# A temperature softmax over 32 x 512 x 1024: the first load in two pieces, and one store by Pool's queue

## The chip, the cores and the metric

The kernel runs on one core of one Trainium2 chip. The metric is the device time in microseconds (us) of one execution. The kernel before takes 317.71 us, the median of three runs (317.61 to 318.15).

## The reference

```python
batch, seq, dim = 32, 512, 1024      # x is float32, temperature is 0.5
def reference(x, temperature):
    scaled = x / temperature
    shifted = scaled - np.max(scaled, axis=-1, keepdims=True)
    exp_x = np.exp(shifted)
    return (exp_x / np.sum(exp_x, axis=-1, keepdims=True)).astype(np.float32)
```

It is a softmax over rows of 1024 numbers, 16,384 rows in all. Input and output are 67.11 MB each, and both have to pass through the core once.

## The kernel before, in words

The rows are cut into 16 tiles. A tile has 1024 rows, eight on each of the 128 partitions of the on-chip memory: 4 MiB. In memory the eight rows of a partition lie one after the other, so that a partition's part of a transfer is one run of 32,768 bytes. Six buffers hold tiles (BUFS = 6, L11), and each tile is worked on in place. It has two groups of four rows per partition (GROUP = 4, L13), 32 groups in all.

For a group, `maximum` (L64) finds the largest element of each row on DVE (L70, one instruction for four rows) and turns it into a bias (L73). `exponential` (L75) computes exp(scale * x + bias) on ACT, a row per instruction with the sum of the row beside it (L79). `divide` (L88) takes the reciprocals of the sums (L91) and multiplies the rows by them on DVE (L93). `store` (L97), after the second group of a tile, sends the tile to memory and calls `load` (L57) for the tile six further on, which takes the buffer that comes free.

Two things set the order of the work:

- The order of instructions on each engine is the order in which the program issues them (L107, a schedule by hand). First come six loads. Then for each group g: maximum and exponential of g, division of g - 1, store of g - 1. So on DVE the maximum of a group stands ahead of the division of the group before it. The division of a tile's second group therefore comes after the maximum over the first group of the next tile, which needs that tile to be loaded.
- All loads are issued by SP (L61). The seventh and later ones wait for a store to land, since they fill the buffer which it empties. All stores are issued by ACT (L101), between its exponentials. Each of the two issuing engines has a queue of its own to the 16 DMA engines, and each DMA engine serves both queues.

Pool (GpSimd) does nothing in this kernel but write four constants at the start.

Of the kernel before, what the change touches and what calls it, by code (L numbers as in the profile page):

```python
# [1 line left out]

# [4 lines left out]

TILES = [[8]] * 16  # L10
BUFS = 6  # L11

GROUP = 4  # L13


@with_exitstack
def kernel(
    ctx: ExitStack,
    tc: tile.TileContext,
    x: bass.AP,  # L20
    temperature: bass.AP,
    out: bass.AP,
):
    nc = tc.nc
    f32 = mybir.dt.float32
    scale = 1.0 / float(temperature)
    extreme = mybir.AluOpType.max if scale > 0 else mybir.AluOpType.min

    P = 128
    xf = x.flatten_outer_dims()  # L30
    of = out.flatten_outer_dims()
    n, d = xf.shape
    assert sum(sum(ks) for ks in TILES) * P == n

    data = ctx.enter_context(tc.tile_pool(name="data", bufs=BUFS))
    stats = ctx.enter_context(tc.tile_pool(name="stats", bufs=4))


    groups, first, r = [], [], 0
    for i, ks in enumerate(TILES):  # L40
        first.append(r)
        r += sum(ks)
        a = 0
        for k in ks:
            for b in range(0, k, GROUP):
                m = min(GROUP, k - b)
                groups.append((i, a + b, m, (a, k) if b + m == k else None))
            a += k

    def dram(t, i):  # L50
        k = sum(TILES[i])
        block = t[P * first[i] : P * (first[i] + k), :]
        return block.rearrange("(p k) d -> p k d", p=P, k=k)

    tiles, small = [], []

    def load():  # L57
        i = len(tiles)
        if i < len(TILES):
            xt = data.tile([P, sum(TILES[i]), d], f32, name="xt")  # L60
            nc.sync.dma_start(out=xt, in_=dram(xf, i))  # L61
            tiles.append(xt)

    def maximum(g):  # L64
        i, a, k, _ = groups[g]
        top, bias, sums, recip = (
            stats.tile([P, k], f32, name=name) for name in ("top", "bias", "sums", "recip")
        )
        small.append((bias, sums, recip))
        nc.vector.tensor_reduce(  # L70
            out=top, in_=tiles[i][:, a : a + k, :], axis=mybir.AxisListType.X, op=extreme
        )
        nc.vector.tensor_scalar_mul(bias, in0=top, scalar1=-scale)  # L73

    def exponential(g):  # L75
        i, a, k, _ = groups[g]
        bias, sums, _ = small[g]
        for b in range(k):
            nc.scalar.activation(  # L79
                tiles[i][:, a + b, :],  # L80
                tiles[i][:, a + b, :],
                mybir.ActivationFunctionType.Exp,
                bias=bias[:, b : b + 1],
                scale=scale,
                accum_out=sums[:, b : b + 1],
            )

    def divide(g):  # L88
        i, a, k, _ = groups[g]
        _, sums, recip = small[g]  # L90
        nc.vector.reciprocal(recip, sums)  # L91
        for b in range(k):
            nc.vector.tensor_scalar_mul(  # L93
                tiles[i][:, a + b, :], in0=tiles[i][:, a + b, :], scalar1=recip[:, b : b + 1]
            )

    def store(g):  # L97
        i, _, _, part = groups[g]
        if part:
            a, k = part  # L100
            nc.scalar.dma_start(out=dram(of, i)[:, a : a + k, :], in_=tiles[i][:, a : a + k, :])  # L101
            if a + k == sum(TILES[i]):
                load()

    with tc.manual_schedule():  # L107

        nc.vector.addr_align(128, offset=0, max_nops=0)
        nc.scalar.addr_align(128, offset=0, max_nops=0)  # L110
        for _ in range(BUFS):
            load()
        for g in range(len(groups) + 1):
            if g < len(groups):
                maximum(g)
                exponential(g)
            if g > 0:
                divide(g - 1)
                store(g - 1)


# [1 line left out]
_INS = ['x', 'temperature']  # L123
_OUTS = [((32, 512, 1024), 'float32')]

_NUMBERS = {'temperature': 0.5}


# [26 lines left out]
```

## Time and profile before

| | |
|---|---|
| median of three runs | 317.71 us |
| the profiled execution's own time | 317.42 us |
| its span, from first to last instruction | 315.6 us |
| DVE busy | 235.5 us (75%) |
| ACT busy | 149.6 us (47%) |
| Pool busy | 0.2 us |
| bytes read and written | 67.11 MB and 67.11 MB, 425 GB/s over the span |
| a load, from issue to landing | 12.7 us at least, 50.2 us in the median |
| a store, from issue to landing | 12.8 us at least, 38.4 us in the median |
| L70, the maximum of a group | 32 times, 4416 ns each |
| L93, a division of a row per partition | 128 times, 749 ns each |
| L79, an exponential of a row per partition | 128 times, 1137 ns each |

The span runs from the first to the last instruction; the device time has 1.8 us more around it. A line such as L61 is a line of the kernel's file. "Issue" of a DMA is the moment at which the engine hands it to its queue; "landing" is when its last byte is there and the waiting engines are told. A row of the waits gives the engine and line that waited, what it waited for, the sum in us, how often, and the longest. A row of the time order gives the start in us, the duration, engine, line, operation, and in brackets the idle time before it and what ended it. A row of the stretches gives the stretch, its length, the busy time of DVE, ACT and Pool with the number of instructions, the clock, the mean busy share of the 16 DMA engines and GB/s. Queue q1 is SP's, q10 is ACT's.

### The profile page before, as it was taken

Reading aid. Unit: us, or ns where it says so; the run is one execution under the profiler, and the core shown is the slowest. Engines: PE = TensorE matmul, PEld = TensorE weight load, DVE = VectorE, ACT = ScalarE, POOL = GpSimd, SP = SyncE. Lnnn points to the kernel's source line nnn. Section 1 sums busy time; section 2 is a strip of 40 time slices with the busy share of each in tenths; the row PEclk is TensorE's granted clock in tenths of the full one; section 3 lists DMA queues with packets and bytes.
Section 4 is the critical chain, followed back from the end, with each engine's and each line's share of the span. In section 5 each row is a group of like instructions: output and inputs, shape, how many; then the busy total and the mean of one; then the engine's idle time right before and its main releaser. Section 6 shows DMA issues by size and latency. Waiting matters only on the chain.

```text
span 315.6 us, 622 instructions
## 1 busy us (share of the span) xinstructions
DVE 235.5 (75%) x224; ACT 149.6 (47%) x257; POOL 0.2 (0%) x4
## 2 busy tenths in 40 slices
DVE  0299999999789494994939949498594976949720
ACT  0176666666626255361553615546065560645500
POOL 0000000000000000000000000000000000000000
DMA  8999999999999999999999999999999999999996
GB/s 330 415 448 415 386 457 407 461 411 453 424 440 432 432 432 429 444 424 453 415 454 407 457 407 457 403 461 403 461 403 461 403 462 403 461 419 444 428 436 278
DMA packets 4613, 134.26 MB, mean 425 GB/s; under 512 B 512, under 2 KB 512, under 8 KB 512
## 3 DMA queue, kind: packets, MB, share of 16 engines
q1 hardware_dynamic: 2304, 67.11, 49.7%
q10 hardware_dynamic: 2304, 67.11, 49.2%
q14 instruction: 5, 0.04, 0.0%
HBM read 67.11 MB, written 67.11 MB: 425 GB/s over the span
## 4 chain that ended last, share of the span: by engine, by line
DVE 72%; another core or an unknown queue 15%; DMA 4%; ACT 3%; issue 1%; DVEq 0%
DVE top L70 43%; DVE xt L93 27%; DMA xt<-in_x_dram 4%; ACT xt L79 3%; DVE recip L91 1%; DVE bias L73 1%; DVEq L150 0%
## 5 line engine op out<-in xcount | busy, mean ns | idle before, releaser
L79 ACT ACTIVATE xt<-xt,bias 128x1024 f32<-128x1024 f32 x128 | 145.4, 1137 | 136.0 <-DVE recip L91 118.6
L70 DVE TENSOR_REDUCE top<-xt 128x4 f32<-128x4096 f32 x32 | 141.3, 4416 | 62.2 <-DMA xt<-in_x_dram 62.2
L93 DVE TENSOR_SCALAR xt<-xt,recip 128x1024 f32<-128x1024 f32 x128 | 87.7, 749 | 1.1
L79 ACT ACTIVATION_READ_ACCUMULATOR xt<-xt,bias 128x1 f32 x128 | 23.8, 186 | 0.0
L79 ACT ACT_TABLE_LOAD x1 | 1.3, 1283 | 13.5 <-DMA xt<-in_x_dram 13.5
L91 DVE RECIPROCAL recip<-sums 128x4 f32<-128x4 f32 x32 | 5.5, 171 | 2.1 <-ACT xt L79 2.1
L73 DVE TENSOR_SCALAR bias<-top 128x4 f32<-128x4 f32 x32 | 5.5, 170 | 1.1
L136 POOL MEMSET const-bfloat16-1.0<- 128x1 bf16 x1 | 0.1, 102 | 0.0
L136 POOL MEMSET const-uint8-127<- 128x1 uint8 x1 | 0.1, 102 | 0.0
L136 POOL MEMSET const-float32-0.0<- 128x1 f32 x1 | 0.1, 99 | 0.2 <-issue 0.2
L136 POOL MEMSET const-float32-1.0<- 128x1 f32 x1 | 0.1, 99 | 0.0
## 6 DMA issues: line engine op xcount, KB each, us to landing
xt<-in_x_dram SPq DMA_DIRECT2D x16, 4096.0 KB, 50.2
out_dram<-xt ACTq DMA_DIRECT2D x16, 4096.0 KB, 38.4
```

The costliest lines, as they stand in the source:

```text
L70: nc.vector.tensor_reduce(out=top, in_=tiles[i][:, a : a + k, :], axis=mybir.AxisListType.X, op=extreme)
L73: nc.vector.tensor_scalar_mul(bias, in0=top, scalar1=-scale)
L79: nc.scalar.activation(tiles[i][:, a + b, :], tiles[i][:, a + b, :], mybir.ActivationFunctionType.Exp, bias=bias[:, b : b + 1], scale=scal ...
L91: nc.vector.reciprocal(recip, sums)
L93: nc.vector.tensor_scalar_mul(tiles[i][:, a + b, :], in0=tiles[i][:, a + b, :], scalar1=recip[:, b : b + 1])
L136: nc = _bacc.Bacc("TRN2", target_bir_lowering=False, num_devices=1)
```

## The change

Two edits. The load of tile 0 becomes two DMAs on SP's queue: one of partitions 0 to 15 (512 KiB), then one of partitions 16 to 127 (3.5 MiB). What needs tile 0 waits for both. The other 15 loads stay as they are. And the store of tile 8, one of 16, is issued by Pool's queue instead of ACT's; the wait for the last division of tile 8 goes with it. The load of tile 14, which takes tile 8's buffer, stays on SP and waits for that store to land, as before.

```diff
 GROUP = 4
+
+BY_POOL = 8
...
             xt = data.tile([P, sum(TILES[i]), d], f32, name="xt")
-            nc.sync.dma_start(out=xt, in_=dram(xf, i))
+
+            for p, q in ((0, 16), (16, P)) if i == 0 else ((0, P),):
+                nc.sync.dma_start(out=xt[p:q], in_=dram(xf, i)[p:q])
             tiles.append(xt)
...
         if part:
             a, k = part
-            nc.scalar.dma_start(out=dram(of, i)[:, a : a + k, :], in_=tiles[i][:, a : a + k, :])
+
+            queue = nc.gpsimd if i == BY_POOL else nc.scalar
+            queue.dma_start(out=dram(of, i)[:, a : a + k, :], in_=tiles[i][:, a : a + k, :])
             if a + k == sum(TILES[i]):
                 load()
```

## The prediction

> **What bounds the kernel now.** I read the DMA rows of the page first, then the stretches, then the waits, then the time order around tile 8 and at the end. The page:
>
> ```profile
> DMA  8999999999999999999999999999999999999996
> ...
> q1 hardware_dynamic: 2304, 67.11, 49.7%
> q10 hardware_dynamic: 2304, 67.11, 49.2%
> ```
>
> The reader is to see that the DMA engines have no free tenth between the first slice and the last. Loads are q1 (SP's queue), stores q10 (ACT's). Each queue has 2048 data packets of 32,768 B (67.11 MB) and 256 small completions. A store packet takes 49.2% x 16 x 315.6 us / 2048 = 1.213 us. An engine carries 256 packets in all: 256 x 1.213 = 310.5 us of a span of 315.6 us. The stretches say the same, with the share of the DMA engines in the last but one column:
>
> ```profile
> 0.00:2.00 2.00, 0.00 (x0) 0.00 (x0) 0.20 (x4) 1.00 0.61 168
> 2.00:33.00 31.00, 19.23 (x16) 13.18 (x22) 0.00 (x0) 1.00 1.00 427
> 33.00:173.00 140.00, 117.03 (x113) 73.62 (x127) 0.00 (x0) 1.00 1.00 431
> 173.00:282.00 109.00, 81.58 (x78) 53.49 (x94) 0.00 (x0) 1.00 1.00 433
> 282.00:302.00 20.00, 17.65 (x19) 9.27 (x16) 0.00 (x0) 1.00 0.97 419
> 302.00:313.00 11.00, 0.00 (x0) 0.00 (x0) 0.00 (x0) 1.00 0.99 429
> 313.00:316.00 3.00, 0.00 (x0) 0.00 (x0) 0.00 (x0) 1.00 0.08 33
> ```
>
> The waits show that the compute engines have time to spare in the long middle, and that what they lack is loaded tiles:
>
> ```profile
> DVE top L70 <- DMA xt<-in_x_dram: 62.2, 12, 13.4
> ```
>
> The first of these 12 waits (13.4 us) is the start; the others are 3 to 5 us, once a tile, from 84.8 us on. In the time order around tile 8:
>
> ```profile
> 173.65 0.34 ACTq L101 DMA_DIRECT2D out_dram<-xt  x1
> 173.91 19.67 SPq L61 DMA_DIRECT2D xt<-in_x_dram  x2
> ...
> 185.48 4.42 DVE L70 TENSOR_REDUCE top<-xt 128x4 f32<-128x4096 f32 x1 [4.48 <-DMA xt<-in_x_dram]
> ...
> 193.00 0.34 ACTq L101 DMA_DIRECT2D out_dram<-xt  x1
> ```
>
> The store of tile 8 is issued at 173.65 us; the load of tile 12 follows at 173.91 us, when the store of tile 6 has landed; tile 10 lands at 185.46; the store of tile 9 goes out at 193.00, 7.54 us after that landing. A store goes out 7.54 us after the landing of a later tile (store 9 after tile 10), since L70 of tile i+1 stands before the last division of tile i. Landings follow every 19.35 us, which is 16 packets of 1.213 us: one load packet, one store packet, in turn. At 173.65 store 7 has its whole tile still to send, so ACT's queue holds one full store in reserve. And the end:
>
> ```profile
> 282.25 4.42 DVE L70 TENSOR_REDUCE top<-xt 128x4 f32<-128x4096 f32 x1 [4.49 <-DMA xt<-in_x_dram]
> ...
> 302.01 0.34 ACTq L101 DMA_DIRECT2D out_dram<-xt  x1
> ```
>
> The last tile is there at 282.2, its store goes out 19.8 us later and lands 12.8 us after that (the least of all stores). So there are two bounds that almost coincide: the DMA work, which ends at 313 to 314.5 us, and the last load plus 33.4 us (315.6 - 282.25). The reserve of stores covers the DMA engines after the last load; nothing is left over. Whatever makes the last load later makes the end later.
>
> [...] The trace shows about 1.0 us for SP (issue at 0.73, first packet at 1.74); nothing of Pool's.
>
> **The change, part by part.** The sum is made against the profiled execution, 317.42 us: its span of 315.6 and 1.8 outside. It lies 0.1% below the median, 317.71.
>
> *The split of the first load.* One more issue on SP, 0.33 us (the row of L61 has 327 ns at least). Loads 1 to 5 are issued later by that, hidden under tile 0's 9.7 us of packets (8 x 1.213); uncovered it would cost 0.33. The 16 more completions are 4 bytes each: nothing. [...] Together 5.7 us, an estimate. Nothing takes it back, since the engines have no free time later: loads, stores and end move by it. Lower bound: zero, if packets are dealt by destination, so that engines not concerned go on with the 112 partitions. Below zero at most about 0.3 us, from a shorter first issue (0.52 against 0.33 us shown, the first of them cold). [...] I take 5.7.
>
> *The store of tile 8 on Pool's queue.* ACT loses one issue of 0.34 us, in a stretch where it waits 7.3 us a tile for DVE: worth nothing. Pool has 0.2 us of work in the whole span, so its wait for the division holds up nobody behind it. Its issue and descriptor work are not shown: [...] a late start only moves the same packets. The first of DVE's next operations is L70, 4.41 us, so nothing short is needed there.
> But it is moved past the store of tile 7: on ACT's queue it would wait behind it; on its own it sends at once. For its 8 packets an engine has three queues in turn, and a load packet comes every 3.64 instead of 2.43 us. Over 8 turns loads fall behind by 8 x 1.213 = 9.7 us. Tile 10 lands some 4.2 us late (3.5 packets left, each 1.21 later), tile 11 at 204.8 + 9.7 = 214.5. Stores come forward instead: store 7 ends about 201.9, store 9 follows directly, has 7 packets left when store 8 is done at 204, and ends at 204 + 7 x 2.43 = 221.3. Store 10 goes out at 214.5 + 7.54 = 222.0 and sends from 223.0. So ACT's queue is empty for 1.7 us, in which loads have the engines alone and win 1.7 us back. 8.0 us remain: store 11 goes out at 224.2 + 8.0 + 7.5 = 239.7 and store 10 is busy till 242.4, so both queues stay filled and the lag is carried to the last load, 290.2. Then the reserve is missing: store 13 ends at about 295, store 14 goes out at 290.2 + 7.5 = 297.7. The engines stand idle about 4 us, and again 2.5 us ahead of the last store. The chain gives the last load + 33.4 = 323.6 span, +8.0 us. Landing of store 8 at 205 rather than 212.6 lets load 14 be issued sooner, behind two others: worth nothing. Bounds: zero, if Pool's packets are served only when another queue is empty and tile 14 is not delayed; above, if they are small and take small turns: a ninth of a turn makes 64 turns of 2.6 us, the load of tile 14 waits for that landing, and the end comes at about +12.5. I take 8.0.
>
> Sum: 317.42 + 5.7 + 8.0 = 331.1 us.
>
> **The rivals.**
> *Pool only.* Packets dealt by destination, the split free: 317.4 + 8.0 = 325.4. [...]
> *Split only.* Pool's queue costs the loads nothing: 317.4 + 5.7 = 323.1. For it: nothing of Pool's is shown. Against: the equal turns of the other two queues.
> *Faster.* The engines do not end together: after 313 us a share of 0.08 over 3 us remains, and the packet records end between 313.3 and 314.5 us, so the last engine is one packet behind, and every landing waits for it. If the stretch in which ACT's queue is empty lets that engine catch up on loads, the last landing comes one packet sooner: 317.4 - 1.2 = 316.2. [...]
> *No change*, 317.4: Pool's packets come late and the split is free.
>
> **How the numbers follow.** Both costs 0.47 (329 to 335, with small turns of Pool's); Pool only 0.22; split only 0.14 (321 to 326); faster 0.08; no change 0.09, of which 0.06 within 0.2% and 0.03 slower. 0.2% is about what a measurement of this kernel tells from no change. So slower 0.47 + 0.22 + 0.14 + 0.03 = 0.86. The range leaves out faster, no change and the lowest of split only: 321.5 to 335.
>
> **What would show it.** Split: first landing (L70's first start, now 13.42) at 17 to 22 us, and tile 0's packets longer than 1.213 us; at 13.4 the split is free. Pool: three queues in the table; waits of L70 of 8 to 10 us for tiles 10 and 11 after 173 us, 4.5 again later; DMA tenths under 9 after the last load. If L70 keeps its 4.5 us and the last slices stay full, my step on turns is wrong. The prediction falls if both are so.

## The result, and the profile after

The changed kernel takes 329.77 us (median of five runs, 329.73 to 330.17), the kernel before 317.61 us beside it: a ratio of 1.0384, interval 1.037 to 1.0398. The forecast was 331.1. The profiled execution took 329.73 us with a span of 328.0, 12.4 us more than the span before.

The DMA rows of the page, kernel after:

```profile
DMA  8999999999999999999999999999999999997877
...
q1 hardware_dynamic: 2320, 67.11, 50.2%
q10 hardware_dynamic: 2160, 62.92, 44.5%
q0 software_dynamic: 144, 4.19, 3.0%
```

Two things have changed. The last four figures of the row are 7 and 8: engines stand idle there, where before only the last figure was below 8. And q1, the loads, took 50.2% of 328.0 us, 164.7 us per engine, where it was 49.7% of 315.6, 156.9 us, for the same bytes: load packets became 7.8 us longer in sum. Pool's queue q0 carries 144 packets, 128 of 32,768 B and 16 completions, so its packets have the size of the others; 3.0% of 328.0 us over 8 packets per engine is 1.23 us each, about the 1.213 of theirs.

The stretches of the kernel after (DMA share and GB/s in the last two columns):

```profile
2.00:8.00 6.00, 0.00 (x0) 0.00 (x0) 0.00 (x0) 1.00 0.81 132
8.00:22.00 14.00, 0.00 (x0) 0.00 (x0) 0.00 (x0) 1.00 0.99 269
22.00:173.00 151.00, 129.47 (x121) 84.64 (x145) 0.00 (x0) 1.00 1.00 433
...
296.00:316.00 20.00, 17.65 (x19) 9.27 (x16) 0.00 (x0) 1.00 0.75 323
316.00:328.00 12.00, 0.00 (x0) 0.00 (x0) 0.00 (x0) 1.00 0.82 350
```

From 8 to 22 us the engines are busy the whole time and move 269 GB/s instead of 427: not idle, but slow. From 296 to 316 us the packets have their usual length (1.216 us in the median) and the engines are idle a quarter of the time. So there are two costs of two kinds, one seen at each end of the kernel.

The time order, kernel after:

```profile
22.43 4.42 DVE L74 TENSOR_REDUCE top<-xt 128x4 f32<-128x4096 f32 x1 [22.43 <-DMA xt<-in_x_dram]
...
173.60 4.42 DVE L74 TENSOR_REDUCE top<-xt 128x4 f32<-128x4096 f32 x1 [4.49 <-DMA xt<-in_x_dram]
...
196.58 4.42 DVE L74 TENSOR_REDUCE top<-xt 128x4 f32<-128x4096 f32 x1 [8.11 <-DMA xt<-in_x_dram]
...
221.96 4.42 DVE L74 TENSOR_REDUCE top<-xt 128x4 f32<-128x4096 f32 x1 [10.52 <-DMA xt<-in_x_dram]
...
296.22 4.42 DVE L74 TENSOR_REDUCE top<-xt 128x4 f32<-128x4096 f32 x1 [4.46 <-DMA xt<-in_x_dram]
...
315.98 0.34 ACTq L107 DMA_DIRECT2D out_dram<-xt  x1
```

L74 here is L70 of before. These are the first maxima of tiles 0, 9, 10, 11 and 15, and the issue of the last store. Against before (13.42, 166.13, 185.48, 204.83, 282.25 us) they are late by 9.0, 7.5, 11.1, 17.1 and 14.0 us. The first lag is the split's. Pool's store, issued at 181.38 us, adds 3.6 at tile 10 and 9.6 at tile 11; later some of it is won back. From the last load to the end of the span are 31.8 us, 1.6 fewer than before: 14.0 - 1.6 = 12.4.

### The profile page after: what moved, and what is told of

It is laid out like the page before. It is cut to its first block, busy times and chain, and to the rows that moved or that the text cites. A ratio compares the mean times of both kernels' runs of the same rounds, so it can differ in the third digit from the quotient of the medians.

```text
span 328.0 us, 625 instructions
## 1 busy us (share of the span) xinstructions
DVE 235.5 (72%) x224; ACT 149.6 (46%) x257; POOL 0.9 (0%) x5
## 3 DMA queue, kind: packets, MB, share of 16 engines
q1 hardware_dynamic: 2320, 67.11, 50.2%
## 4 chain that ended last, share of the span: by engine, by line
DVE 48%; DMA 36%; another core or an unknown queue 8%; ACT 3%; issue 1%; DVEq 0%; SPq 0%
DVE top L74 29%; DMA xt<-in_x_dram 21%; DVE xt L97 17%; DMA out_dram<-xt 15%; ACT xt L83 3%; DVE bias L77 1%; DVE recip L95 1%; DVEq L156 0%; SPq L65 0%; DVEq L74 0%
## 5 line engine op out<-in xcount | busy, mean ns | idle before, releaser
L74 DVE TENSOR_REDUCE top<-xt 128x4 f32<-128x4096 f32 x32 | 141.3, 4416 | 76.1 <-DMA xt<-in_x_dram 76.1
L83 ACT ACT_TABLE_LOAD x1 | 1.3, 1283 | 22.4 <-DMA xt<-in_x_dram 22.4
L107 POOL DMA_DIRECT2D out_dram<-xt x1 | 0.7, 655 | 180.9 <-DVE xt L97 180.9
## 6 DMA issues: line engine op xcount, KB each, us to landing
xt<-in_x_dram SPq DMA_DIRECT2D x1, 3584.0 KB, 21.2
```

The lines of the kernel that those rows point to most:

```text
L74: nc.vector.tensor_reduce(out=top, in_=tiles[i][:, a : a + k, :], axis=mybir.AxisListType.X, op=extreme)
L83: nc.scalar.activation(tiles[i][:, a + b, :], tiles[i][:, a + b, :], mybir.ActivationFunctionType.Exp, bias=bias[:, b : b + 1], scale=scal ...
L107: queue.dma_start(out=dram(of, i)[:, a : a + k, :], in_=tiles[i][:, a : a + k, :])
```

## The experiments

**One part at a time, and two other cuts of the first load.** e1 has only the split, by setting the number of the tile that goes by Pool to none.

```diff
-BY_POOL = 8
+BY_POOL = None
```

> Only the split of the first load (16 and 112 partitions); all stores by ACT. [...] the packets of tile 0 last longer, as in the changed kernel, where the loads' packets took 7.8 us more per DMA engine (50.2% of 328.0 us against 49.7% of 315.6), and nothing takes it back: 317.6 + 7.8 = 325.4 us, first maximum at about 22.4 us, waits of L74 4.5 us in the middle. The prediction's own figure was 323.1. Rival, the two edits only hurt together (the split costs its place in time, the lag vanishes once stores begin): under 320.

Measured: 325.51 us against 317.9, ratio 1.0233 (1.0218 to 1.0249), +7.6. The last load is 8.0 us late, as tile 9 is already 7.8 us late: what the start costs is not given back.

e2 has only the store by Pool.

```diff
-            for p, q in ((0, 16), (16, P)) if i == 0 else ((0, P),):
+            for p, q in ((0, 16), (16, P)) if False else ((0, P),):
```

> Only the store of tile 8 by Pool; the first load whole. Turns theory: loads fall behind by some 9.7 us while three queues take turns, win 1.7 to 4 us back while ACT's queue is empty, and the last load lands 6 to 8 us late; the last store finds its queue empty and lands about 1.7 us sooner after its issue: 317.6 + 4.4 to 6.5 = 322 to 324. Rival, Pool's path itself costs (descriptor work and a late first packet): loads keep their times, only the landing of store 8 is late, and the end stays within 1 us of 317.6.

Measured: 322.22 us, ratio 1.0129 (1.0114 to 1.0145), +4.3. The product of the two ratios is 1.0365, a little under the lower end of the interval for both together, 1.037: the parts add up to within 0.2%. The time order of e2:

```profile
174.16 0.66 POOL L107 DMA_DIRECT2D out_dram<-xt  x1 [173.71 <-DVE xt L97]
189.34 4.42 DVE L74 TENSOR_REDUCE top<-xt 128x4 f32<-128x4096 f32 x1 [8.09 <-DMA xt<-in_x_dram]
196.85 0.34 ACTq L107 DMA_DIRECT2D out_dram<-xt  x1
214.72 4.42 DVE L74 TENSOR_REDUCE top<-xt 128x4 f32<-128x4096 f32 x1 [10.51 <-DMA xt<-in_x_dram]
222.23 0.34 ACTq L107 DMA_DIRECT2D out_dram<-xt  x1
230.45 4.42 DVE L74 TENSOR_REDUCE top<-xt 128x4 f32<-128x4096 f32 x1 [0.87 <-DMA xt<-in_x_dram]
...
288.92 4.42 DVE L74 TENSOR_REDUCE top<-xt 128x4 f32<-128x4096 f32 x1 [4.48 <-DMA xt<-in_x_dram]
```

Tile 11 is 9.9 us late (214.72 - 204.83), tile 12 only 6.3 (230.45 - 224.19), the last 6.7. So the rival in which loads keep their times falls. What gives 3.6 us back between tiles 11 and 12 is seen in the DMA view of 222 to 225.5 us, kernel e2 (queue, packets, MB, and their time as a share of the 16 engines; it can pass 100%, since a packet counts whole where it begins):

```profile
q1 hardware_dynamic: 48, 1.57, 104.4%
```

Loads alone, though ACT issued a store at 222.23: its packets are not there yet.

e3 cuts the first load at the same sizes, but along the rows, so that each piece has all partitions. It is made from the kernel before.

```diff
-            nc.sync.dma_start(out=xt, in_=dram(xf, i))
+            for p, q in ((0, 1), (1, 8)) if i == 0 else ((0, 8),):
+                nc.sync.dma_start(out=xt[:, p:q, :], in_=dram(xf, i)[:, p:q, :])
```

> The first load in two DMAs of the same sizes as in the change (512 KiB and 3.5 MiB), but cut along the rows: row 0 of each of the 128 partitions, then rows 1 to 7. All stores by ACT. [...] packets of 4 KiB and 28 KiB take their share of 1.213 us, and the time is 317.6 within 0.6. Rival, a second DMA for the first tile costs by itself (issue, descriptors, completion, the wait for two landings): as slow as the 16 and 112 split, about 325.

Measured: 318.55 us, ratio 1.0022 (1.0014 to 1.003). That is a little outside the 0.6 us that I had allowed. A second DMA costs 0.7 us, not 7.6: that the cut runs through the partitions is what matters.

e4 cuts it into two halves of 64 partitions.

```diff
-BY_POOL = 8
+BY_POOL = None
...
-            for p, q in ((0, 16), (16, P)) if i == 0 else ((0, P),):
+            for p, q in ((0, 64), (64, P)) if i == 0 else ((0, P),):
```

> The first load as partitions 0 to 63 and then 64 to 127. All stores by ACT. [...] four packets each at half rate, one half after the other on every engine: 8 x 2.43 in place of 8 x 1.21, a loss of up to 9.7 us, 325 to 327.5, though the halves are equal and large. Rival, the cost comes from the small piece of 16 partitions: nothing here, 317.6 to 318.5. Rival, packets are dealt by destination: nothing here either.

Measured: 327.17 us, ratio 1.0286 (1.0269 to 1.0304), +9.3, in the range. Kernel e4, page (each figure is for a fortieth of the span, 8.1 us):

```profile
GB/s 195 193 258 419 419 451 447 399 443 451 419 423 447 451 395 443 448 439 411 443 447 412 427 447 447 403 443 447 419 427 443 447 400 443 447 439 411 443 447 270
```

195 and 193 GB/s while tile 0 comes in, less than half of the 427 that the kernel before moved from 2 to 33 us. Half the rate was an assumption of mine that no earlier trace showed; the figures here meet it. Both rivals expected nothing, the one of the small piece and the one of packets dealt by destination, and both fall, and "Pool only" with the second. What slows a piece of 64 partitions was not shown: no run here separates the on-chip side from the main memory, where a cut by partitions also narrows the region that is read at a time.

**Pool's queue at other places.** In e5 tile 2 goes by Pool, in e6 the last one, in e7 all; the first load is whole in each, as in e2.

```diff
-BY_POOL = 8
+BY_POOL = 2          # e5
+BY_POOL = 15         # e6
...
-            queue = nc.gpsimd if i == BY_POOL else nc.scalar
+            queue = nc.gpsimd if True else nc.scalar   # e7
```

> First load whole; the store of tile 2 instead of tile 8 goes by Pool, some 110 us earlier, where DVE does not yet wait for loads. Turns theory: loads fall behind by a packet per turn all the same, ACT's reserve of one store is gone for the rest of the span, and nothing restores it: about as slow as with tile 8, 321 to 323.5, with empty DMA slices after the last load. Rival, the lag is worked off in the 240 us that follow: within 1.5 us of 317.7.

Measured: 326.45 us, ratio 1.0278 (1.0248 to 1.0307), +8.7: not worked off in 240 us, but also twice the cost of tile 8, and above my range. The landing records of the trace (16 times for each transfer, which I read as one for the part of each DMA engine) show where the rest comes from. The first engine has its part of the last load there at 285.4 us, 5.9 late, about as in e2 (6.1). But thirteen parts are there by 287.6, and the last three only at 290.7, 292.7 and 292.8; DVE's first maximum of tile 15 starts at 292.87. So two engines are about six packets behind the first in loads, a third somewhat less, and the landing waited for the slowest. In e2 the first and the slowest are 3.3 us apart, before 2.7. What puts these engines so far back was not found.

> First load whole; only the store of the last tile goes by Pool. No load is left that it could delay, so turns cost nothing. What remains is Pool's own path: its first packet came 5.8 us after the issue in the run with tile 8 alone (with busy engines), against 0.9 us for a store of ACT with idle engines. Turns theory: 317.7 + 1 to 5 us, by the late first packet alone. Rival, a store by Pool costs the same wherever it stands: 322.2.

Measured: 317.97 us, ratio 1.001 (1.0002 to 1.0019). With no load left to delay, a store by Pool costs 0.2 us, less than the 1 to 5 that I had expected: Pool's first packet came 1.2 us after its issue here (302.75 to 303.97), not 5.8.

> First load whole; all 16 stores by Pool, none by ACT. Turns theory: then there are again two queues in turn, and a reserve on Pool's queue as before on ACT's. The loads keep their times (last one at about 282), and only the last store's late first packet shows: as with the last tile alone, 318.5 to 322.5. Rival, Pool's path costs per store (descriptors, landing): 16 times as much as one, over 330.

Measured: 319.02 us, ratio 1.004 (1.0025 to 1.0055). Sixteen stores by Pool cost 1.3 us, in the range and less than a third of what one costs between ACT's. So Pool's path itself is nearly free; a second queue of stores beside the first is what costs.

**A split load in the middle.** e8, in e1:

```diff
-            for p, q in ((0, 16), (16, P)) if i == 0 else ((0, P),):
+            for p, q in ((0, 16), (16, P)) if i == 10 else ((0, P),):
```

> All stores by ACT; the load of tile 10 instead of tile 0 is cut into 16 and 112 partitions. [...] the packets of that load last longer wherever it stands[...] the loss is the same or somewhat less: 317.7 + 4 to 8 us. Rival, the cost belongs to the start (cold first packets, nothing else queued): within 1 us of 317.7.

Measured: 322.13 us, ratio 1.0135 (1.012 to 1.0151), +4.4, in the lower part of the range. The cost does not belong to the start. It is smaller beside stores, of which it lengthens few: q1 is 50.0% and q10 48.7% of 320.5 us, together 316.3, 4.2 us more than the 312.1 of before (3.4 of it loads, 0.8 stores).

**Several stores, and the sign turned.** e9 sends the stores of all even tiles by Pool (in e2's kernel), e10 sends one load by Pool and no store (in the kernel before), e11 the store of tile 8 and the load that follows into its buffer (in e2's kernel).

```diff
-            queue = nc.gpsimd if i == BY_POOL else nc.scalar
+            queue = nc.gpsimd if i % 2 == 0 else nc.scalar          # e9
...
-            nc.sync.dma_start(out=xt, in_=dram(xf, i))
+            queue = nc.gpsimd if i == 12 else nc.sync               # e10
+            queue.dma_start(out=xt, in_=dram(xf, i))
...
-                nc.sync.dma_start(out=xt[p:q], in_=dram(xf, i)[p:q])
+                queue = nc.gpsimd if i == 14 else nc.sync           # e11
+                queue.dma_start(out=xt[p:q], in_=dram(xf, i)[p:q])
```

> First load whole; the stores of all eight even tiles go by Pool, the odd ones by ACT. Turns theory: what a store by Pool takes from the loads is ACT's reserve of waiting stores, and that can be lost once; stores cannot run further ahead than the tiles that are finished. So little more than with one tile: 322 to 327. Rival, each store by a second queue costs its 4.4 us again: 8 x 4.4 = 35 us, about 353.

Measured: 331.49 us (328.62 to 333.49), ratio 1.0421 (1.0359 to 1.0482): far from the 353 of the rival, but 4.5 us above my range. In the landing records the first engine has the last load at 279.2 us, as before (279.5), the slowest at 299.9, 20.7 us later. Nine of the 16 parts are there by 279.6, so on those engines the loads are not late at all; the whole delay is that of the engines that have fallen behind, five of them by 12 us and more. A lag of all engines alike, lost once as I had expected, does not show here: e9 refutes the rival, but its own cost comes from engines that drift apart, as in e5, and why they do stays open.

> All stores by ACT; the load of tile 12 goes by Pool's queue. Turns theory with the sign turned: for eight turns loads have two of three turns, so loads come forward, stores fall back and wait in ACT's queue; the DMA engines stay full to the end, which the amount of work sets: 317.0 to 318.7. Rival, a third queue costs by itself: 322.

Measured: 317.83 us, ratio 1.0002 (0.9993 to 1.001). A third queue costs nothing when it carries this load. Tiles 10 and 11 are as late as in e2 (their waits are 8.1 and 10.6 us), since SP's queue loses turns all the same, but tile 12 is already there, DVE works through the rest without a further wait, and the last store goes out at 293.61 us, 8.4 us sooner than before. The DMA engines are then full to the end, as the page and the time order of kernel e10 show, and the amount of DMA work sets it:

```profile
DMA  8999999999999999999999999999999999999996
...
293.61 0.34 ACTq L102 DMA_DIRECT2D out_dram<-xt  x1
```

> First load whole; the store of tile 8 by Pool as in the change, and the load of tile 14, which follows it into the same buffer, by Pool too. Turns theory: the load gives back on Pool's queue the turns that the store took, the last load lands some 6 us sooner than with the store alone, and the end comes back to 317.7 to 319.5. Rival, costs of Pool's queue add up: 322 or more.

Measured: 322.69 us, ratio 1.0168 (1.013 to 1.0206). My expectation failed, and the number lies where the rival had it. Kernel e11, time order:

```profile
243.57 4.42 DVE L75 TENSOR_REDUCE top<-xt 128x4 f32<-128x4096 f32 x1 [12.99 <-DMA xt<-in_x_dram]
259.32 4.42 DVE L75 TENSOR_REDUCE top<-xt 128x4 f32<-128x4096 f32 x1 [0.88 <-DMA xt<-in_x_dram]
...
308.62 0.34 ACTq L108 DMA_DIRECT2D out_dram<-xt  x1
```

The loads did come forward: DVE waits for none after tile 13 (259.32), and the last landing is at 279.1 us, 3 us sooner than before. But the load by Pool took its turns from tile 12, which DVE needs first and got at 243.57, 19.4 us later than before. From there DVE's own work is the chain: stores follow every 14.8 us up to that of tile 14, and the last goes out at 308.62, as late as in e2 (308.68). So I read the 322.69 as the order of the loads and not as costs of Pool's queue that add up: e10's load by Pool cost nothing. No run tries that order by itself. Turns given to a later tile do not help when DVE has too few tiles left to catch up.

**The cut through the partitions by itself.** e12 cuts the first load into eight pieces of 16 partitions, in e1's kernel.

```diff
-            for p, q in ((0, 16), (16, P)) if i == 0 else ((0, P),):
+            for p, q in [(p, p + 16) for p in range(0, P, 16)] if i == 0 else ((0, P),):
```

> All stores by ACT; the first load in eight pieces of 16 partitions. [...] the whole tile comes at a quarter of the rate: 8 x 4.85 = 38.8 us in place of 9.7, +29: 347 (343 to 348, if engines drift apart and pieces overlap). Rival, the cost is that of one small piece at the start, or of seven packets per engine over 112 partitions: 325 or less.

Measured: 343.47 us, ratio 1.0806 (1.0785 to 1.0827), +25.75, at the lower end of the range. Kernel e12, stretches and queue:

```profile
2.00:10.00 8.00, 0.00 (x0) 0.00 (x0) 0.00 (x0) 1.00 0.92 108
10.00:20.00 10.00, 0.00 (x0) 0.00 (x0) 0.00 (x0) 1.00 1.12 128
20.00:30.00 10.00, 0.00 (x0) 0.00 (x0) 0.00 (x0) 1.00 0.94 108
```

```profile
q1 hardware_dynamic: 2416, 67.11, 53.4%
```

108, 128 and 108 GB/s in these stretches, where the kernel before moved 427 from 2 to 33 us, and pieces land every 4.54 us by the landing records (524,288 B in 4.54 us are 115 GB/s): the quarter of the rate, which I had assumed without a run to show it (4 x 1.213 = 4.85 us a piece), is about what came. 2416 packets are 2048 of data and 368 = 23 x 16 completions for 23 loads, so a piece of 16 partitions has 16 completions, like a whole load. In the changed kernel the first 16 load packets begin between 1.75 and 3.02 us and none ends before 4.50, so they are under way together: I read that a piece of 16 partitions runs on all 16 engines.

## Why the prediction was right, and which terms were off

The bound was read rightly: the DMA engines had no free time, and the last load plus a tail of DVE's work and one store closed the span. Both edits act through these two, e1 and e2 show each alone, and neither changed anything else: DVE and ACT are busy 235.5 and 149.6 us before and after. The forecast of 13.7 us stands against 12.2 measured. That it is so close is luck: two terms were off in opposite directions, by 1.9 and 3.7 us.

*The split: 5.7 forecast, 7.6 measured.* The forecast was 3.64 us for the piece of 16 partitions and 2.1 for that of 112. Both rested on an assumption of how much a cut through the partitions slows a packet, which the trace of before, with loads of 128 partitions alone, does not show. For the piece of 16, e12's 4.54 us a piece gives 4.54 - 1.21 = 3.3. The mis-sized term is that of the 112 partitions: of the 7.8 us by which q1 grew, 4.5 are left for it, an estimate (the two pieces overlap in the trace, and its packet records put still more on the 112). The forecast had 4 engines of 16 at half rate and the others at full rate. The trace has no packet at full rate: each of the 110 load packets that begin between 8 and 21.2 us took 1.4 us or more, half of them 1.8 to 2.1, against 1.213. Why stays open. The first maximum came at 22.4 us, just past the 17 to 22 forecast.

The extra issue on SP was costed at 0.33 us, hidden. It was more: SP waited 3.8 us for the landing of the first piece before the last of its first loads went out (at 8.2 us). It was hidden all the same, behind loads already queued.

*The store by Pool: 8.0 forecast, 4.3 measured.* The lag of 9.7 us by eight turns was met (9.9 at tile 11), and in e2 the store of tile 10 went out at 222.23 for a forecast 222.0. Then two terms failed. The first: "sends from 223.0", so that ACT's queue would be empty 1.7 us. In e2 the first packet of that store came at 225.97 us, and loads won back 3.6 us instead of 1.7. I had taken 1.0 us from the very first load, with idle engines; the trace of before had the better row in it. The store of tile 0 is issued there at 33.12 us, and its DMA view of 33 to 37 us has only this, kernel before:

```profile
q1 hardware_dynamic: 47, 1.54, 107.2%
```

The second: the tail of 33.4 us was carried over unchanged. It holds a store that waits for the end of the one before it (12.8 us to its landing). With engines idle ahead of it, it lands after 11.1 us, and the tail is 31.8. So 9.9 - 3.6 = 6.3, 6.7 at the last load, less 1.6: 5.1 us in e2's profiled execution, 4.3 by the medians.

Of the rivals, "Pool only" falls by e1, e4 and e12, "split only" by e2. "Faster" needed the two costs under 1.2 us together. "No change" falls with them.

## What to carry to other kernels

Where the DMA engines are full from start to end, cut a transfer along what keeps all 128 partitions in each piece: the same two sizes cost 0.7 us cut by rows (e3) and 7.6 cut by partitions (e1). And while loads still follow, do not put one store of a stream on a queue of its own: it overtakes nothing that matters, and takes turns from the loads (4.3 us for the one of tile 8, 0.2 for the last, 1.3 for all sixteen together). To price a new queue, take the time from issue to first packet from a row in which the engines are as busy as they will be.

## What the runs showed of the hardware that I had not expected

- A queue that was empty gets its first packet late while loads keep the engines busy: ACT's store of tile 0 before 4.0 us after its issue (33.12 to 37.1), the store at 222.23 us in e2 3.7 us, Pool's there 5.8 (174.16 to 179.98). In e6, where the loads were over and ACT's queue was at its last packets, Pool's took 1.2 us (302.75 to 303.97). With idle engines the last store of e2 took 0.8 us (308.68 to 309.5).
- In the runs with stores on two queues beside the loads, the 16 engines can drift apart: in e9 the parts of one load landed over 20.7 us, before over 2.7.
